# Eight conditioning jobs of layer 1 from VectorE to TensorE, TensorE held in program order through attention, and layer 0's scaled input kept in PSUM

## The chip, the cores and the metric

The kernel runs on one core of one Trainium2 chip. A time is the device time of one execution in microseconds; the kernel before took 926.71 us (median of 3 runs, 925.51 to 928.1). TensorE (PE), VectorE (DVE), ScalarE (ACT) and GpSimd (POOL) each run their own instructions strictly in the order in which they were laid down; SyncE (SP) issues the DMAs, also in order.

## The reference

One sample of 256 tokens of width 2048 goes through two layers. Every layer scales and shifts its normed input by vectors computed from a conditioning vector `c`, and gates its output by a third:

```python
mod = sc @ ada_w[layer] + ada_b[layer]            # sc = silu(c); 2048 x 6144
shift, scale, gate = jnp.split(mod[:, None, :], 3, axis=-1)
h = modulate(rmsnorm(x, norm_g[layer]), shift, scale)
...
k, v, q, za, glu, zb = jnp.split(h @ w_in, EV_SPLITS, axis=-1)      # layer 0
q = apply_rope(rmsnorm(q, ev_q_norm[e]), cos, sin)
k = apply_rope(rmsnorm(k, ev_k_norm[e]), cos, sin)
attn = latent_attention(q, k, v, kc, vc)          # kc, vc: the same weights on 256 context tokens
conv = conformer_conv(glu, ...)                   # 31 taps, LayerNorm, swish
mix = concatenate([attn * silu(za), conv * silu(zb)])
x = x + gate * (mix @ ev_w_out[e])
...
p = h @ od_w_in[o]                                # layer 1: spatial gating, SiLU gate
x = x + gate * ((spatial_gating(p[..., :2*SGU_W], ...) * silu(p[..., 2*SGU_W:])) @ od_w_out[o])
```

The output is the RMS-normed `x`.

## The kernel before, in words

All large products are done in two-part precision: weight and input are each split into a high part in a short format and the remainder, and three matmuls (high by high, high by low, low by high) stand for one. Weights stream from HBM in pieces of 512 KB. One piece is a **job** of kind W (`w_job`, line 347): a DMA into one of ten ring buffers `raw`; ACT makes the high part `whi` (line 361); POOL or DVE makes the remainder `wlo` (line 364; POOL for jobs 30 to 133, `P0` and `P1`); PE multiplies, 24 matmuls of 256 columns for a job of `w_rows` (lines 386 to 389), 12 of 512 columns for one of `w_cols` (409 to 411), 48 of 256 for keys and values (560 to 564). There are four `whi` and four `wlo` buffers, and a job is split up to four W jobs ahead. The sums stand in PSUM banks of tag `acc`, three of them, taken in turn; a helper, `part` (line 527), adds them into SBUF on DVE.

Jobs of kind A compute the conditioning vectors. Some run on PE (`adan_jobs`, line 289: matmuls against the 32-column `ccol`, ended by `ada_fin`, a copy on ACT, a transpose and an addition on DVE). The others run on DVE (`adat_jobs`, line 255): two SCALAR_TENSOR_TENSOR instructions on each 512 KB of transposed weights `traw`, against a copy of `c` in PSUM (line 274).

`make_h` (line 443) makes the layer's input for a group of rows: on DVE `ht` = x times scale times the norm's factor (line 453), on ACT the high part `h` = `ht` + shift (line 456), on DVE the remainder (line 460). `prep_x` does it for the tokens, `prep_c` for the context, in layer 0 in groups of 2 or 4 blocks of 128 rows; `prep1` does it for layer 1 once its norm is known.

Attention is a list of small **steps** (`side["attn"]`) put between the W jobs by `drain`. `rope_q` (line 753) takes the sum of squares of each query head (ACT, line 720), its reciprocal root (`rsqrt`, line 222), and rotates the unscaled queries on DVE (lines 709 to 714); the factor is applied later, in the soft-max. `attn_head` (line 773) is S = q k (line 776), the row maximum on DVE (779), its product with the factor (780), the exponential on ACT (782), a reciprocal (783) and a scaling on ACT (785). `attn_tr` (line 790) transposes that on PE (796) and copies it on ACT (797); `attn_pv` (line 801) multiplies with the values for two heads (807). S stands in the one bank of tag `S`, and once the flag `q` is set, every second one in an `acc` bank. The convolution's taps (line 626) are steps of a second list, all on DVE.

The order of each engine's instructions is not the program's: a scheduler lays them out from modelled times, and may move an instruction past others of its engine when the data allow it. `tc.high_priority()` and `tc.issue_after()` bend that; the DMAs alone are kept in the program's order.

Of the kernel before, what the change touches and what calls it, by code (L numbers as in the profile page):

```python
# [11 lines left out]
F32 = mybir.dt.float32  # L12
# [5 lines left out]
D = 2048  # L18
# [26 lines left out]
P2 = 4  # L45
# [32 lines left out]
NBLK = [(0, kind * D + k0 * 128, n * 128) for k0, n in GROUPS for kind in range(2)]  # L78
# [7 lines left out]
def backbone_kernel(  # L86
# [146 lines left out]


# [7 lines left out]
    def adat_pair(l, ca, cb_):  # L242

        ja, jb = adat_jobs(l, ca), adat_jobs(l, cb_)
        return [j for u in range(4) for js in (ja, jb) for j in js[4 * u : 4 * u + 4]]
# [9 lines left out]
    def adat_jobs(l, c0):  # L255

        js = []
# [3 lines left out]
        for u, q in enumerate(order):  # L261
            for t in range(4):
# [7 lines left out]
                def mm(jb=jb, t=t, q=q, u=u):  # L270
# [99 lines left out]
    def w_rows(jobs, src, kbs, h, post):  # L370
# [3 lines left out]
        for n, (kq, kts) in enumerate(parts):  # L374
            def mmf(jb, kq=kq, n=n, kts=kts):
# [3 lines left out]
                for kt in kts:  # L379
                    hh, hl = h(kq * 4 + kt)  # L380
                    k = kt - kts[0]
                    for b in range(2):
# [3 lines left out]
                        nc.tensor.matmul(o, wh, hh, start=(n == 0 and kt == kts[0] and b == 0), stop=False,  # L386
                                         skip_group_check=True)
                        nc.tensor.matmul(o, wh, hl, start=False, stop=False, skip_group_check=True)  # L388
                        nc.tensor.matmul(o, wl, hh, start=False, stop=end, skip_group_check=True)  # L389
# [4 lines left out]
    def w_cols(jobs, src_f, kbs, hs, post):  # L394
# [3 lines left out]
        for n, (kp, kts) in enumerate(parts):  # L398
            def mmf(jb, kp=kp, n=n, kts=kts):
# [3 lines left out]
                for i, (h, ch) in enumerate(hs):  # L403
                    for k, kt in enumerate(kts):
# [4 lines left out]
                        nc.tensor.matmul(accs[i], hh[:, sl], jb.hi[:, k, :], start=s0, stop=False)  # L409
                        nc.tensor.matmul(accs[i], hh[:, sl], jb.lo[:, k, :], start=False, stop=False)  # L410
                        nc.tensor.matmul(accs[i], hl[:, sl], jb.hi[:, k, :], start=False, stop=s1)  # L411
# [122 lines left out]
    turns = []  # L534

    def two_steps(first, second):

        side["attn"].append(first)
        if turns:
# [652 lines left out]
```

## Time and profile before

| | |
|---|---|
| median of 3 runs | 926.71 us |
| the profiled execution | 926.46 us, of which the profile's span is 924.7 us |
| PE busy | 872.9 us (94%) |
| DVE busy | 659.6 us (71%) |
| ACT busy | 457.9 us (50%) |
| POOL busy | 258.6 us (28%) |
| mean granted PE clock | 0.975 |

A busy time counts what an engine works, not what it waits. PE is near full in most of the span; it is not before 40 us, from 160 to 200, from 280 to 340, from 420 to 540 and behind 900 us. In a row of the windows view the numbers are busy microseconds and, in brackets, instructions of each engine in that stretch, then the granted PE clock as a share of full speed, the busy share of the DMA engines and GB/s. In the chain of waits each row is a piece of the path back from the last instruction: start, length, engine and what it wrote, with the line. In the view of groups, "busy, mean ns | idle before" stands behind each group of like instructions. "PEld" is PE's weight load.

### The profile page before, as it was taken

The numbers are of one execution on the slowest core, as the hardware profiler recorded it, in microseconds if no ns is written. First come the engines' busy times: TensorE is split into PE (matmuls) and PEld (weight loads), VectorE is DVE, ScalarE is ACT, GpSimd is POOL, SyncE is SP. The second block draws the span as 40 slices with busy tenths as digits, with TensorE's granted clock in tenths as the row PEclk, the third lists the DMA queues.
The fourth block names the chain that finished last, engine by engine and source line by source line (L and its number), as shares of the span: only waits on it lengthen the run. The fifth ranks groups of instructions, "written<-read, shape, count | busy, mean of one in ns | idle before, by whom it ended". The sixth has DMA issues, their size and how long they took to land.

```text
span 924.7 us, 17928 instructions
## 1 busy us (share of the span) xinstructions
PE 872.9 (94%) x7084; PEld 800.5 (87%) x7084; DVE 659.6 (71%) x1413; ACT 457.9 (50%) x648; POOL 258.6 (28%) x125
## 2 busy tenths in 40 slices
PE   5999999599998689999999899999999999999994
PEld 3798899599887578998999778998899999999994
DVE  2355684978887877895765299998988977554442
ACT  5643242347557668545544544455583544444441
POOL 0000023659875235686777520000000000000000
PEclk9999999799999899999999899999999999999998
DMA  9999999685776332678889579988887788755402
GB/s 355 406 389 352 363 338 365 252 286 173 233 247 217 121 114 91 205 249 298 312 311 342 175 277 410 409 312 304 311 281 225 250 282 281 218 185 174 137 1 91
DMA packets 66864, 239.06 MB, mean 259 GB/s; under 512 B 7502, under 2 KB 7768, under 8 KB 66268
## 3 DMA queue, kind: packets, MB, share of 16 engines
q1 hardware_dynamic: 66780, 237.92, 72.9%
q8 instruction: 55, 0.90, 0.4%
q14 instruction: 29, 0.24, 0.1%
HBM read 235.80 MB, written 2.10 MB: 257 GB/s over the span
## 4 chain that ended last, share of the span: by engine, by line
PE 76%; DVE 10%; DMA 10%; ACT 3%; issue 1%; POOL 0%; SPq 0%; DVEq 0%; POOLq 0%; ACTq 0%
PE acc L386 17%; PE acc L389 16%; PE acc L388 16%; DMA traw<-adat 7%; PE acc L409 4%; PE acc L410 4%; PE acc L411 4%; DVE traw L274 4%; PE ada L317 3%; PE acc L560 2%; PE acc L562 2%; PE acc L564 2%; DVE conv L626 1%; DMA braw<-ada 1%; PE rms L191 1%
## 5 line engine op out<-in xcount | busy, mean ns | idle before, releaser
L361 ACT ACTIVATE whi<-raw 128x1024 fp32r<-128x1024 f32 (+1 forms) x256 | 263.4, 1031 | 285.1 <-PE acc L388 140.4
L364 POOL TENSOR_TENSOR wlo<-raw,whi 128x1024 fp32r<-128x1024 f32 x104 | 250.9, 2425 | 283.3 <-ACT whi L361 145.4
L364 DVE TENSOR_TENSOR wlo<-raw,whi 128x1024 fp32r<-128x1024 f32 (+1 forms) x152 | 176.8, 1165 | 83.3 <-ACT whi L361 81.7
L274 DVE SCALAR_TENSOR_TENSOR traw<-traw,cbp 128x512 f32<-128x512 f32 x256 | 165.3, 682 | 56.0 <-DMA traw<-adat 52.7
L386 PE MATMUL acc<-h,whi 128*128 128x256 f32 x512 | 152.4, 299 | 8.0 <-DVE gaT L532 6.7
L388 PE MATMUL acc<-h,whi 128*128 128x256 f32 x512 | 149.3, 293 | 0.4 <-DVE h L460 0.4
L389 PE MATMUL acc<-h,wlo 128*128 128x256 f32 x512 | 148.0, 290 | 1.6 <-POOL wlo L364 1.6
L388 PE MATMUL acc<-h1l,whi 128*128 128x256 f32 x512 | 145.2, 284 | 0.0
L389 PE MATMUL acc<-h1h,wlo 128*128 128x256 f32 x512 | 145.0, 283 | 0.0
L386 PE MATMUL acc<-h1h,whi 128*128 128x256 f32 x512 | 145.0, 283 | 0.0
L626 DVE SCALAR_TENSOR_TENSOR conv<-gaT,small,conv 128x241 f32<-128x241 f32 (+14 forms) x240 | 114.6, 478 | 5.2
L386 PEld LDWEIGHTS acc<-h,whi 128*128 128x128 f32 x512 | 100.6, 197 | 14.1 <-issue 10.3
L389 PEld LDWEIGHTS acc<-h,wlo 128*128 128x128 f32 x512 | 100.5, 197 | 4.1 <-issue 2.0
L388 PEld LDWEIGHTS acc<-h,whi 128*128 128x128 f32 x512 | 100.7, 197 | 3.5 <-issue 2.6
L388 PEld LDWEIGHTS acc<-h1l,whi 128*128 128x128 f32 x512 | 98.2, 192 | 0.1
L386 PEld LDWEIGHTS acc<-h1h,whi 128*128 128x128 f32 x512 | 98.2, 192 | 0.1
L389 PEld LDWEIGHTS acc<-h1h,wlo 128*128 128x128 f32 x512 | 98.2, 192 | 0.0
L389 PE MATMUL acc<-m1h,wlo 128*128 128x256 f32 x256 | 73.1, 286 | 0.0
L386 PE MATMUL acc<-m1h,whi 128*128 128x256 f32 x256 | 72.4, 283 | 0.0
L388 PE MATMUL acc<-m1l,whi 128*128 128x256 f32 x256 | 72.4, 283 | 0.0
L389 PEld LDWEIGHTS acc<-m1h,wlo 128*128 128x128 f32 x256 | 49.1, 192 | 2.9 <-issue 2.9
L411 PE MATMUL acc<-whi,h1l 128*128 128x512 f32 x128 | 51.1, 400 | 0.0
(235 smaller groups left out, 1649.1 us busy)
## 6 DMA issues: line engine op xcount, KB each, us to landing
traw<-adat SPq DMA_DIRECT2D x128, 512.0 KB, 5.0
raw<-w_out SPq DMA_DIRECT2D x64, 512.0 KB, 4.0
raw<-w_uz SPq DMA_DIRECT2D x64, 512.0 KB, 4.9
araw<-ada SPq DMA_DIRECT2D x56, 512.0 KB, 6.9
raw<-w_gate SPq DMA_DIRECT2D x56, 512.0 KB, 5.1
raw<-w_v SPq DMA_DIRECT2D x32, 512.0 KB, 5.1
raw<-w_q SPq DMA_DIRECT2D x16, 512.0 KB, 4.1
raw<-w_gate SPq DMA_DIRECT2D x16, 256.0 KB, 11.0
```

The costliest lines, as they stand in the source:

```text
L274: nc.vector.scalar_tensor_tensor(out=jb.raw[:, k, :], in0=jb.raw[:, k, :], scalar=1.0, in1=cbq["t"], op0=ALU.mult, op1=ALU.mult, accum_out ...
L317: nc.tensor.matmul(st8["p"][32 * g : 32 * g + 32, :w], ccol[:, kb, :], jb.raw[:, a, q * w : (q + 1) * w], start=kb < 4 // nq, stop=kb >= N ...
L361: nc.scalar.activation(hv, jb.raw, AF.Copy)
L364: eng.tensor_tensor(out=jb.lo.rearrange("p a b -> p (a b)"), in0=jb.raw, in1=hv.bitcast(F32), op=ALU.subtract)
L386: nc.tensor.matmul(o, wh, hh, start=(n == 0 and kt == kts[0] and b == 0), stop=False, skip_group_check=True)
L388: nc.tensor.matmul(o, wh, hl, start=False, stop=False, skip_group_check=True)
L389: nc.tensor.matmul(o, wl, hh, start=False, stop=end, skip_group_check=True)
L409: nc.tensor.matmul(accs[i], hh[:, sl], jb.hi[:, k, :], start=s0, stop=False)
L410: nc.tensor.matmul(accs[i], hh[:, sl], jb.lo[:, k, :], start=False, stop=False)
L411: nc.tensor.matmul(accs[i], hl[:, sl], jb.hi[:, k, :], start=False, stop=s1)
L560: nc.tensor.matmul(o, hh[:, sl], jb.hi[:, k, :], start=kq == kqs[0] and k == 0 and c == 0, stop=False, skip_group_check=True)
L626: nc.vector.scalar_tensor_tensor(out=o, in0=y, scalar=w, in1=o, op0=ALU.mult, op1=ALU.add)
```

## The change

Four things are changed together.

1. **Conditioning.** The shift vector's blocks 8 to 11 of layer 1 (columns 1024 to 1535) are no longer computed on DVE. They were 8 of the 32 DVE jobs of `ada1b` (`ts=range(2, 4)` leaves t = 2 and 3) and are now 8 jobs of `adan_jobs` on PE, behind the hook of `prep1(0)`, the norm of layer 1.
2. **PE's order.** Matmuls and transposes of W jobs and of attention go through `inorder`, which ties each to the one before it, from the first query job up to layer 1's norm. Attention's list is rewritten for that: one `unit` between two W jobs holds S of head n, the value product of two earlier heads and the transpose of head n - 3, all with high priority, and the two transposes of queries are steps of their own. The first two W jobs behind the queries take no step (`rest`).
3. **Scaled queries.** `rope_q` scales the queries in PSUM on ACT (four instructions for 4 heads), as the keys already were; the rotation works in place with one SBUF temporary at a time. The soft-max loses the factor: the maximum is negated in the reduction, and line 780 goes.
4. **Scaled input.** In layer 0 `make_h` puts `ht` in a PSUM bank (tag `m`, two banks) in place of SBUF.

```diff
-NBLK = [(0, kind * D + k0 * 128, n * 128) for k0, n in GROUPS for kind in range(2)]
+NBLK = [(0, kind * D + k0 * 128, n * 128) for k0, n in GROUPS for kind in range(2)] + [(1, 1024, 512)]
...
+    def inorder(op, *args, **kw):
+
+        with tc.issue_after(pe["last"]) if pe["on"] and "last" in pe else nullcontext():
+            i = op(*args, **kw)
+        pe["last"] = i.ins
...
-            t = tmp.tile([128, 2, T], F32, tag="t2", name="ht", bufs=TB)
+            if m == 4:
+                t = bank("ht").rearrange("p (a b) -> p a b", a=2)
+            else:
+                t = tmp.tile([128, 2, T], F32, tag="t2", name="ht", bufs=TB)
...
-        at["rq"][i, cg] = head_rstd(src, 4, "qss", HD ** -0.5)
+        r = head_rstd(src, 4, "qss", HD ** -0.5)
+        for h in range(4):
+            nc.scalar.activation(src[:, h * 128 : (h + 1) * 128], src[:, h * 128 : (h + 1) * 128], AF.Copy, scale=r[:, h : h + 1])
...
-        nc.vector.tensor_reduce(out=mx[:, 0:1], in_=S, axis=AX.X, op=ALU.max)
-        nc.vector.tensor_scalar(out=mx[:, 1:2], in0=mx[:, 0:1], scalar1=rq, scalar2=-1.0, op0=ALU.mult, op1=ALU.mult)
+        nc.vector.tensor_reduce(out=mx[:, 1:2], in_=S, axis=AX.X, op=ALU.max, negate=True)
...
+        def unit(n):
+
+            if n < len(todo):
+                attn_head(*todo[n])
+            if n > AD and (n - AD) % 2 == 0:
+                attn_pv(*todo[n - AD - 1])
+            if AD <= n < len(todo) + AD:
+                attn_tr(*todo[n - AD])
+        for n in range(len(todo) + AD + 1):
             if n == len(todo) // 2:
-                half = len(out)
...
+                out.append(("q", both(turn_q, 1)))
+            out.append(lambda n=n: unit(n))
+        return out + [("za", attn_gate), lambda: attn_fin(0), lambda: attn_fin(1)]
...
-    segs = [body, qa + kv[0] + za[:4] + qb, kv[1] + za[4:] + [za_ready], z_part(1) + [conv_tail], [need("attn")] + o0a, [need("conv")] + o0b]
+    segs = [body, [hook(lambda: pe.__setitem__("on", True))] + qa + za[:2] + kv[0] + za[2:4] + qb + [hook(lambda: st.__setitem__("rest", 2))], za[4:8] + kv[1] + za[8:] + [za_ready], z_part(1) + [conv_tail], [need("attn")] + o0a, [need("conv")] + o0b]
...
-    ada1b = adat_pair(1, 1024, D + 1024)
-    plan += [hook(lambda: prep1(0)), hook(sgu_const)]
+    ada1b = adat_pair(1, 1024, D + 1024, range(2, 4))
+    plan += [hook(lambda: pe.__setitem__("on", False)), hook(lambda: prep1(0))] + adan_jobs(1, 1024, 512) + [hook(sgu_const)]
```

Three places in the built order show where instructions went. The first is DVE at the last `prep_x` and `prep_c` of layer 0 (blocks 12 to 15; line 453 or 470 is `ht`, 460 or 477 the remainder of tokens (`h_2267`) and context (`hc`), 274 or 287 conditioning, 532 or 549 the emptying of an `acc` bank). Before:

```order
L453 SCALAR_TENSOR_TENSOR ht<-xT_71,modv_133,rB_223 128x256 x4
L453 SCALAR_TENSOR_TENSOR ht<-cT_325,modc,rBc 128x256 x4
L274 SCALAR_TENSOR_TENSOR traw,adat<-traw,cbp 128x512 x2
L532 TENSOR_TENSOR kv_sb<-acc,kv_sb 128x2x256
L460 SCALAR_TENSOR_TENSOR h_2267<-ht,modv_133,h_2267 128x256
L274 SCALAR_TENSOR_TENSOR traw,adat<-traw,cbp 128x512 x2
L460 SCALAR_TENSOR_TENSOR h_2267<-ht,modv_133,h_2267 128x256 x3
L460 SCALAR_TENSOR_TENSOR hc<-ht,modc,hc 128x256
L532 TENSOR_TENSOR gaT<-acc,gaT 128x512
```

And in the changed kernel, from the second pair of token blocks on:

```order
L470 SCALAR_TENSOR_TENSOR ht<-xT_71,modv_133,rB_223 128x256 x2
L287 SCALAR_TENSOR_TENSOR traw,adat<-traw,cbp 128x512 x3
L549 TENSOR_TENSOR gaT<-acc,gaT 128x512
L287 SCALAR_TENSOR_TENSOR traw,adat<-traw,cbp 128x512
L477 SCALAR_TENSOR_TENSOR h_2267<-ht,modv_133,h_2267 128x256 x4
L287 SCALAR_TENSOR_TENSOR traw,adat<-traw,cbp 128x512 x4
L470 SCALAR_TENSOR_TENSOR ht<-cT_325,modc,rBc 128x256
L549 TENSOR_TENSOR gbT<-acc,gbT 128x512
L470 SCALAR_TENSOR_TENSOR ht<-cT_325,modc,rBc 128x256 x3
L477 SCALAR_TENSOR_TENSOR hc<-ht,modc,hc 128x256 x4
L287 SCALAR_TENSOR_TENSOR traw,adat<-traw,cbp 128x512 x2
L549 TENSOR_TENSOR gaT<-acc,gaT 128x512
```

The first emptying of `gaT` now stands ahead of the remainders, the second (the last row) behind those of the context, and the context's `ht` behind the tokens' remainders.

The second is ACT around the second group of queries (`sqj` are the squares, line 767 the new scaling, 222 or 223 the root, 782 or 787 the exponential, 785 or 790 the scaling behind it, 797 or 802 and 815 or 820 copies of transposes and values). Before, the exponentials of S stand between the parts of the query norm, each with a load of its function table:

```order
L720 ACTIVATE sqj,qss<-acc 128x128
L782 ACT_TABLE_LOAD
L782 ACTIVATE P,mx<-S,mx,qss 128x512
L223 ACT_TABLE_LOAD
L223 ACTIVATE qss<-qss,epsc 128x4
L361 ACTIVATE whi<-raw 128x1024
L785 ACTIVATE P<-P,mx 128x512
L815 COPY mixA<-O 128x2x128
L361 ACTIVATE whi<-raw 128x1024
L782 ACT_TABLE_LOAD
L782 ACTIVATE P,mx<-S,mx,qss 128x512
```

In the changed kernel the rows from the fourth square of the second half on; ahead of them stand, behind the last query matmul, the squares x4, a table load, the root, a square, `whi`, a square, a copy of a transpose, a square, a scaling:

```order
L730 ACTIVATE sqj,qss<-acc 128x128
L767 ACTIVATE acc<-acc,qss 128x128
L222 ACTIVATE qss<-qss,epsc 128x4
L767 ACTIVATE acc<-acc,qss 128x128 x2
L375 ACTIVATE whi<-raw 128x1024
L767 ACTIVATE acc<-acc,qss 128x128 x4
L375 ACTIVATE whi<-raw 128x1024 x2
L787 ACT_TABLE_LOAD
L787 ACTIVATE P,mx<-S,mx 128x512
L790 ACTIVATE P<-P,mx 128x512
L787 ACTIVATE P,mx<-S,mx 128x512
```

The exponential of head 6 now stands behind the whole query norm; on PE, S of head 6 comes right behind the last query job, then three W jobs (72 matmuls), then S of head 7, in the same bank.

The third is PE at layer 1's norm (`rms` the sums of squares, `csum_p` and `csum_b` the steps to its factor, `bs_p` constants of the gating unit, `ada` the moved conditioning matmuls). Before:

```order
L191 MATMUL rms_5553<-sq_6086,onesD 32x256 x2
L207 MATMUL csum_p<-q_126,csum 128x1 x2
L212 MATMUL csum_b<-ident,rs 128x128 x2
L170 MATMUL bs_p<-rowh,sel 128x128
L171 MATMUL bs_p<-rowl,sel 128x128
```

Changed:

```order
L331 MATMUL ada_6150<-araw,ccol 32x128 x39
L190 MATMUL rms_5553<-sq_6078,onesD 32x256 x2
L331 MATMUL ada_6150<-araw,ccol 32x128 x22
L206 MATMUL csum_p<-q_126,csum 128x1 x2
L331 MATMUL ada_6150<-araw,ccol 32x128 x3
L211 MATMUL csum_b<-ident,rs 128x128 x2
L347 MATMUL adat<-ident,adar 128x128
L238 MATMUL acc<-whi,h1h 128x512
```

All 64 conditioning matmuls stand in the gaps between the steps of the norm, and the eight `bs_p` moved behind the first four matmuls of the next job.

More of the change, by code (lines that the diff above doesn't have):

```diff
@@ L44 @@
 L1 = 2
-P2 = 4
 NF = 3
@@ L240, in backbone_kernel, with adat_pair @@
         pool = False
-    def adat_pair(l, ca, cb_):
-        ja, jb = adat_jobs(l, ca), adat_jobs(l, cb_)
-        return [j for u in range(4) for js in (ja, jb) for j in js[4 * u : 4 * u + 4]]
+    def adat_pair(l, ca, cb_, ts=range(4)):
+        ja, jb = adat_jobs(l, ca, ts), adat_jobs(l, cb_)
+        return [j for u in range(4) for js in (ja[u], jb[u]) for j in js]
     cbq = {"q": None}
@@ L253, in cb_part, with adat_jobs @@
             nc.vector.tensor_copy(cbq["t"], cb[:, q * 512 : (q + 1) * 512])
-    def adat_jobs(l, c0):
-        js = []
+    def adat_jobs(l, c0, ts=range(4)):
+        js = [[] for _ in range(4)]
         n = TSET.index((l, c0))
@@ L261, in adat_jobs @@
         for u, q in enumerate(order):
-            for t in range(4):
+            for t in ts:
                 jb = Job()
@@ L385, in mmf @@
                         end = n == len(parts) - 1 and kt == kts[-1]
-                        nc.tensor.matmul(o, wh, hh, start=(n == 0 and kt == kts[0] and b == 0), stop=False,
+                        matmul(o, wh, hh, start=(n == 0 and kt == kts[0] and b == 0), stop=False,
                                          skip_group_check=True)
-                        nc.tensor.matmul(o, wh, hl, start=False, stop=False, skip_group_check=True)
-                        nc.tensor.matmul(o, wl, hh, start=False, stop=end, skip_group_check=True)
+                        matmul(o, wh, hl, start=False, stop=False, skip_group_check=True)
+                        matmul(o, wl, hh, start=False, stop=end, skip_group_check=True)
                 if n == len(parts) - 1:
@@ L532, in part @@
             nc.vector.tensor_tensor(out=dst, in0=a, in1=dst if prev is None else prev, op=ALU.add)
[L534 to L539, printed above, removed]
-            side["attn"].append(turns.pop(0))
-        turns.append(second)
     def kv_part(kqs):
@@ L828, in attn_steps, with both @@
     def attn_steps():
-        out, half = [], 0
+        def both(f, *args):
+            return lambda: [f(i, *args) for i in range(2)]
+        out = [both(turn_k), lambda: [turn_k(i) for i in (2, 3)], both(turn_q, 0)]
         todo = [(kvh, c, hq) for kvh in range(NKV) for c in range(2) for hq in range(4)]
-        for n in range(len(todo) + AD):
-            if n == len(todo) // 2:
-                half = len(out)
-            if n < len(todo):
-                out.append(lambda n=n: attn_head(*todo[n]))
-            if n >= AD:
-                out.append(lambda n=n: attn_tr(*todo[n - AD]))
-                if (n - AD) % 2 == 1:
-                    out.append(lambda n=n: attn_pv(*todo[n - AD]))
-        out.append(("za", attn_gate))
-        out += [lambda: attn_fin(0), lambda: attn_fin(1)]
-        return out[:half], out[half:]
+        def unit(n):
[6 more added lines that the diff above has]
+        for n in range(len(todo) + AD + 1):
+            if n == len(todo) // 2:
+                out.append(("q", both(turn_q, 1)))
+            out.append(lambda n=n: unit(n))
+        return out + [("za", attn_gate), lambda: attn_fin(0), lambda: attn_fin(1)]
     def hm(kb):
@@ L1024, in drain @@
             s = side[key].pop(0)
-            (s[1] if isinstance(s, tuple) else s)()
+            with tc.high_priority() if key == "attn" else nullcontext():
+                (s[1] if isinstance(s, tuple) else s)()
             k += 1
@@ L1074, in backbone_kernel @@
         if j.kind == "W":
-            j.pool = P0 <= nw < P1 and nw % 4 < P2
+            j.pool = P0 <= nw < P1
             nw += 1
@@ L1107, in backbone_kernel @@
             for key in ("attn", "conv"):
+                if key == "attn" and st.get("rest"):
+                    st["rest"] -= 1
+                    continue
                 ahead = [n for k, n in deadline.items() if k == key and n > p]
@@ L1110, in backbone_kernel @@
                 for _ in range(math.ceil((PACEA if key == "attn" else PACE) * len(side[key]) / max(1, left))):
-                    if side[key] and isinstance(side[key][0], tuple) and side[key][0][0] == "za" and "za" not in st:
+                    if side[key] and isinstance(side[key][0], tuple) and side[key][0][0] not in st:
                         break
```

78 lines of the change are left out of this document (39 added, 39 removed).

## The prediction

> **What bounds the kernel now.** I read the page's slices first, then the windows around each stretch where PE is not full, then the chain of waits in the two worst, then the groups for durations. In the windows the first pair of numbers is PE's busy time and its matmuls; PEclk and the DMA share stand at the end.
>
> ```profile
> 160.00:200.00 40.00, 30.45 (x218) 29.90 (x216) 33.52 (x60) 15.25 (x20) 23.36 (x10) 0.83 0.73 269
> 200.00:220.00 20.00, 20.00 (x169) 20.00 (x168) 18.10 (x44) 14.24 (x37) 14.29 (x15) 1.00 0.61 195
> 200.00:420.00 220.00, 207.78 (x1372) 185.13 (x1374) 186.19 (x461) 136.67 (x230) 138.80 (x70) 0.97 0.58 191
> 280.00:340.00 60.00, 47.78 (x267) 37.75 (x266) 48.06 (x126) 40.91 (x71) 24.89 (x11) 0.89 0.46 150
> 540.00:900.00 360.00, 360.00 (x2671) 342.48 (x2670) 277.11 (x494) 180.64 (x209) 2.40 (x1) 1.00 0.74 256
> ```
>
> PE is the bound: from 540 to 900 us it has no idle time at all, so nothing that is taken from DVE there can show. The losses lie earlier. At 200 to 220 us PE does 169 matmuls of 256 columns in 20 us, 0.118 us each. From 160 to 200 us it does 218, worth 25.8 us: **14.2 us are lost**, of which 9.55 are idle and the rest is slow clock (0.83). So each idle microsecond cost 1.49. From 280 to 340 us shapes mix and no such count can be made: 12.2 us are idle, the clock (0.89) is worth up to 6.6 more; scaled like the first stretch (14.2 of 9.55 + 6.8) I take **16.5 lost**, bounds 12.2 and 18.8.
>
> The chain of waits in the first stretch, start and length:
>
> ```profile
> 161.54 2.29 DVE modc L344
> ...
> 165.04 3.17 DVE ht L453 x8
> ...
> 169.95 2.50 DVE h L460
> 172.45 1.21 DVE traw L274 x4
> 173.66 6.30 DVE h L460 x3
> 179.97 2.48 DVE hc L460
> 182.45 0.61 DVE gaT L532
> ```
>
> PE waits for none of the remainders here, but for an `acc` bank that `gaT` empties, and `gaT` stands behind five remainders on DVE. Those take 2.1 to 2.5 us each; the same instruction takes a fifth elsewhere. What differs is POOL, which runs five `wlo` at that time:
>
> ```profile
> 169.81 12.35 POOL L364 TENSOR_TENSOR wlo<-raw,whi 128x1024 fp32r<-128x1024 f32 x5 [6.00 <-ACT whi L361]
> ...
> L460 DVE SCALAR_TENSOR_TENSOR h<-ht,modv,h 128x256 fp32r<-128x256 f32 x16 | 16.3, 1056 | 0.1
> L274 DVE SCALAR_TENSOR_TENSOR traw<-traw,cbp 128x512 f32<-128x512 f32 x256 | 165.3, 682 | 56.0 <-DMA traw<-adat 52.7 <-issue 1.4 <-POOL kr L714 0.7
> L453 DVE SCALAR_TENSOR_TENSOR ht<-cT,modc,rBc 128x256 f32<-128x256 f32 x16 | 6.7, 477 | 0.0
> L453 DVE SCALAR_TENSOR_TENSOR ht<-xT,modv,csum_b 128x256 f32<-128x256 f32 x8 | 3.2, 475 | 1.1 <-PE csum_b L212 1.1
> ```
>
> `traw` at 172.45, with one input in SBUF and one in PSUM (`cbp`), keeps its pace while POOL works; the remainder, with both in SBUF, doesn't. One operand in PSUM costs DVE nothing by itself: 475 ns with `csum_b` (PSUM), 477 with `rBc` (SBUF). The Trainium skill (SBUF — State Buffer, "Who interferes with whom") says so as a rule: a VectorE instruction with two SBUF inputs waits for a GpSimd instruction that reads SBUF, one with a single SBUF input does not. By that rule, the trace agrees, 2.50 us for the first remainder and 1.21 for the `traw` pieces behind it, the new remainder is free; `ht`, with two inputs in SBUF, is not (a rival below).
>
> In the second stretch, who PE waited for (us in total, times, longest), and the pieces that PE and ACT work there:
>
> ```profile
> PE S L776 <- ACT P L782: 3.9, 2, 2.3
> PE acc L776 <- ACT z0T L601: 3.0, 1, 3.0
> PE S L776 <- ACT qT L770: 2.6, 1, 2.6
> PE O L807 <- ACT PT L797: 2.6, 1, 2.6
> ...
> 347.23 0.44 PE ptp L796 x4
> 350.78 0.86 PE S L776 x2
> 352.83 1.73 PE O L807 x8
> ...
> L361 ACT ACTIVATE whi<-raw 128x1024 fp32r<-128x1024 f32 x53 | 56.0, 1057 | 49.0 <-PE acc L388 24.4 <-issue 9.7 <-POOL wlo L364 6.5
> L785 ACT ACTIVATE P<-P,mx 128x512 f32<-128x512 f32 x16 | 11.6, 723 | 4.5 <-DVE mx L783 4.5
> L797 ACT COPY PT<-ptp 128x512 f32<-128x512 f32 x16 | 9.3, 582 | 3.2 <-PE ptp L796 3.1
> L782 ACT ACTIVATE P<-S,mx,qss 128x512 f32<-128x512 f32 x11 | 8.5, 776 | 14.2 <-DVE mx L780 14.2
> L782 ACT ACT_TABLE_LOAD x6 | 7.7, 1283 | 0.1
> L720 ACT ACTIVATE sqj<-acc 128x128 f32<-128x128 f32 x16 | 4.4, 274 | 0.9 <-PE acc L411 0.6
> L720 ACT ACTIVATION_READ_ACCUMULATOR sqj<-acc 128x1 f32 x16 | 3.2, 197 | 0.0
> ...
> 244.98 0.28 ACT L720 ACTIVATE sqj<-acc 128x128 f32<-128x128 f32 x1 [0.62 <-PE acc L411]
> 257.89 0.41 DVE L714 TENSOR_TENSOR qr<-rp,rp 128x256 f32<-128x256 f32 x1
> ```
>
> Every wait is for ACT, whose queue alternates between exponential, root and SiLU with 1.28 us of table load at each turn.
>
> **The change part by part.** *Scaled input in PSUM.* The remainder then reads one input from SBUF. The five on the chain (2.50 + 6.30 + 2.48 = 11.3 us) would take some 0.4 us each, 2 us: the 0.48 of `ht` less overlap (3.17 for eight). What is late next? By the new order, with the trace's durations from the transposes at 160 us: `ht` at 164.4 to 167, `gaT` 169.5, the tokens' remainders until 171.8. PE's third job waits about 1.2 us for its `wlo`, and the sixth for the `acc` bank that the second `gaT` empties behind the context's remainders: near 180, 1.4 us of wait, if the context's `ht` (both inputs still in SBUF) is not held up by POOL; near 184, 5.8 us, if POOL's `wlo` hold two of them for 2 us each. Left over: 1.2 + 1.4 = 2.6 us, or (1.2 + 5.8) with clock, some 9. The gain is 11.5 or 5; I take **8**, between them, since POOL worked in most, not all, of that time (23.36 of 40 us).
>
> *PE in order, units, scaled queries.* A unit with its W job fills PE for 24 x 0.118 + 0.86 + 0.44 + 1.73/2 = 5.0 us. ACT needs for the same 1.06 + 0.78 + 0.72 + 0.58, with an accumulator's reading (0.2) and half of a value copy about 3.5 us, and for every fourth job two table loads more, 4.2 us. So PE need not wait in the plain run of units, and the seven units of the first key head have one table load in all. Four places remain. (a) The first queries: from the first square to the last rotation it took 13.3 us (244.98 to 258.3); eight scalings of about 0.28 (by the square's 274) add 2; PE has 15 us of other work ahead of the transposes: 0.5 us. (b) S of head 7 needs the bank of head 6, whose exponential stands behind the second query norm: 8 squares of 0.4 us (274 and 197 ns, overlapping), 4 `whi`, 8 scalings, two roots and a copy of a transpose some 1.2 (0.58 for the copy, the roots an estimate as for a square), two table loads 2.6, the exponential 0.8: 3.2 + 4.2 + 2.2 + 1.2 + 2.6 + 0.8 = 14.2 us from the last query matmul. PE has S, a transpose and 72 matmuls until then: 1.3 + 8.5 = 9.8. It waits 4.4 us, 6.5 with its clock (x 1.49). (c) A new `z` sum wants the `acc` bank which the SiLU empties: a table load 1.3, the SiLU about as long as the copy of 582 ns, a `whi` ahead of it 1.06, less the 1.3 of S and transpose that PE has: 1.5. (d) Others, chosen: 1. Together **9.5 against 16.5: gain 7**. Bounds: nothing waits but (b), gain 12; every unit waits as before, gain 0. The skill's rule on the clock (TensorE: Matmul & The Clock Gate, "What's actually happening") speaks against this part: the array falls to half speed after an idle window of about 3.4 us. By that rule, (b) would cost at most 1.7 us beyond its idle time, an estimate, and the sum be 0.4 us lower than with my 2.1; the clock of 0.83 where 9.55 of 40 us were idle agrees.
>
> ```profile
> L780 DVE TENSOR_SCALAR mx<-mx,qss 128x1 f32<-128x1 f32 x16 | 3.1, 204 | 0.0
> DVE traw L274 <- DMA traw<-adat: 8.0, 9, 1.3
> ...
> 32.68 0.79 PE ada L317 x22
> 38.71 1.01 PE ada L317 x32
> PE rms L191 <- ACT sq L877: 1.6, 1, 1.6
> PE csum_b L212 <- DVE rs L224: 0.6, 1, 0.6
> PE csum_p L207 <- ACT csum L204: 0.5, 1, 0.5
> ```
>
> *Convolution.* DVE loses 16 x 0.204 = 3.3 us with line 780 and must finish its taps on time, as PE sums them right behind attention. From 200 to 420 us DVE is busy for 186 of 220; if PE is 15 us sooner, it has 205 for 183, 89%, with 8.0 us of waiting for the data of nine `traw` on top. The last tap may come late: 0 to 5 us, I take **1.5 of loss**.
>
> *Eight jobs on PE.* 64 matmuls at 1.01 us for 32 are 2.0 us. They stand in waits for the norm of 1.6, 0.5 and 0.6 us, 2.7 together. **Nothing**, while their data is there: without that cover 2 us, and if the eight ring buffers that they hold until then delay the next weights, 2 more. DVE's 16 instructions less (16 x 0.68 = 10.9 us) lie in the stretch without a PE wait and give nothing. The `bs_p` that leave the gap fill the wait for the remainder behind four matmuls: 0, bounds -1 and +1.5.
>
> Sum: 926.5 (profiled execution; span 924.7 and 1.8 around it; median 926.7) - 8 - 7 + 1.5 = **913 us**.
>
> **The rivals.** *The lock moves on.* The context's `ht`, and the next group's, still have two SBUF inputs; each start behind a `wlo` costs up to 2 us, as line 460 now. For it: POOL will have `wlo` queued when they start; against: `ht` ran at 0.47 in every row, because its ACT successors held the `whi` back. First gain 5 in place of 8: 926.5 - 5 - 7 + 1.5 = 916 us. The Trainium skill's rule on two SBUF inputs (SBUF — State Buffer, the section named above) would have it so.
>
> *DVE becomes the bound.* Its taps are laid down with waits for S and DMA among them; if none of its 34 idle us go, PE waits at the sums of the convolution for what it won in attention: 926.5 - 8 = 918.5.
>
> *Slower.* In program order PE cannot step over an S whose bank is taken. If maximum (0.69), `whi` (1.06), scaling (0.72), exponential (0.78) and on DVE a `traw` pair (1.5) with its DMA wait (1.1) stand in a row, the bank is free after 5.85 us; PE's cover from S to S is 5.0 - 0.86 = 4.1. 16 units wait 1.75 each, 28 us, with (b) 34.4 against 16.5: 926.5 + 17.9 - 8 + 1.5 = 938 us. It decides from 1 us per unit on. Against it: DVE has idle time there, and units have high priority.
>
> *No effect.* The waits return elsewhere, for weights: 926. Against it: a DMA share of 0.61 behind the first stretch.
>
> **How the numbers follow.** Forecast 48%, lock 20%, DVE 17%, no effect 8%, slower 7%. A measurement can tell 0.3% (2.8 us) from no change. Forecast, lock and DVE are faster: 0.85; same 0.08; slower 0.07. The range: 901 (the larger ends, 11.5 + 12, with some loss) to 923 leaves out no effect, slower, and a few per cent below.
>
> **What would show it.** Remainders of layer 0 near 0.48 us in the groups; 160 to 200 us with PE above 35 us busy; one wait of S for the exponential of 4 to 5 us behind the second queries; no table load between exponentials before that; the sums of the convolution with PE waiting 1 to 2 us; PE full behind the norm. Wrong, if remainders stay long, if many S wait, or if PE waits for DMA at the norm.

## The result, and the profile after

The changed kernel takes 919.75 us (median of 20 runs, 915.92 to 928.9), the kernel before beside it 927.5 us (20 runs, 924.71 to 933.34). The ratio is 0.9923, with a 95% interval of 0.9903 to 0.9942: some 7 us faster, where 13.5 were predicted. The profiled execution of after took 921.4 us (span 919.5), 1.65 above its median; that of before, 1.04 below its own. So the two traces lie 5.1 us apart and the medians 7.75. Single executions scatter by 3 us and more, and small effects are better read stage by stage than from the totals.

The two traces cut at the same TensorE work, in us between the first starts of the matmuls named (PE's rows in order of time); "hidden products" are the first matmuls behind layer 1's norm:

| stage | before | after | difference | predicted |
|---|---|---|---|---|
| start to the first output matmul of layer 0 | 416.6 | 401.7 | -14.9 | -8 - 7 |
| output matmuls of layer 0 (convolution beside them) | 105.7 | 109.3 | +3.6 | +1.5 |
| norm of layer 1, to the first hidden product | 7.0 | 7.1 | +0.1 | 0 |
| first 32 high-by-high hidden products | 27.1 | 30.6 | +3.5 | 0 |
| the next 111 us of them | 111.4 | 111.4 | 0 | 0 |
| the stretch with the gating matmuls | 145.6 | 148.3 | +2.7 | 0 |
| the rest, to the last matmul | 101.8 | 102.2 | +0.4 | 0 |

The 15 us that were to be won up to the end of attention were won. Ten were lost again behind it, where 1.5 had been allowed for.

The windows of after, PE's busy time and matmuls first, PEclk and the DMA share at the end:

```profile
160.00:200.00 40.00, 35.31 (x278) 34.56 (x277) 35.27 (x80) 18.70 (x29) 27.62 (x12) 0.96 0.90 336
280.00:340.00 60.00, 56.09 (x366) 49.01 (x365) 54.01 (x129) 43.94 (x85) 28.65 (x12) 0.94 0.47 150
298.60:305.30 6.70, 5.87 (x13) 4.02 (x14) 6.70 (x15) 1.50 (x3) 2.47 (x2) 0.50 0.81 290
520.40:527.20 6.80, 6.80 (x20) 5.62 (x21) 6.80 (x15) 3.02 (x7) 2.51 (x1) 0.50 1.03 413
527.20:534.00 6.80, 6.80 (x31) 5.52 (x30) 6.80 (x7) 2.38 (x3) 5.07 (x2) 1.00 0.97 383
660.00:700.00 40.00, 37.80 (x313) 37.23 (x312) 33.07 (x67) 22.88 (x24) 0.00 (x0) 1.00 0.78 250
```

From 160 to 200 us PE does 278 matmuls where it did 218, and from 280 to 340 us it idles 3.9 us where it idled 12.2. But from 660 to 700 us, inside the stretch that had no idle time, it now idles 2.2. Of the signs that the prediction named, one is plainly missing: PE is not full behind the norm.

The groups on DVE that the first term of the sum rests on (a line's mean in ns stands behind its busy time):

```profile
L477 DVE SCALAR_TENSOR_TENSOR h<-ht,modv,h 128x256 fp32r<-128x256 f32 x16 | 6.8, 475 | 1.1 <-ACT h L473 1.1
L470 DVE SCALAR_TENSOR_TENSOR ht<-cT,modc,rBc 128x256 f32<-128x256 f32 x16 | 13.5, 883 | 0.1
L477 DVE SCALAR_TENSOR_TENSOR h1l<-ht,modv,h1h 128x256 fp32r<-128x256 f32 x16 | 13.2, 878 | 0.0
```

The tokens' remainder went from 1056 to 475 ns, and the context's `ht` from 477 to 883: the hold-up has moved one instruction on.

Who PE waited for, from 240 us to the end of attention (402), then from 400 to 530, then from 640 to 720 us (total, times, longest):

```profile
PE S L238 <- ACT P L787: 4.6, 2, 3.9
PE acc L238 <- ACT z0T L609: 1.3, 1, 1.3
PE O L238 <- ACT PT L802: 1.1, 1, 1.1
PE ktp L238 <- ACT kT L759: 1.0, 1, 1.0
...
PE cmean L190 <- ACT gaT L637: 2.3, 1, 2.3
PE acc L238 <- DVE mBl L455: 1.6, 1, 1.6
PE bs_p L169 <- DVE modv L354: 1.1, 1, 1.1
PE acc L238 <- ACT h1h L473: 1.0, 1, 1.0
PE acc L238 <- ACT mBh L454: 0.7, 1, 0.7
...
PE sgu L963 <- DVE mixed L971: 1.4, 1, 1.4
PE sgu L963 <- ACT v L936: 0.7, 1, 0.7
```

In attention stand the waits that were foretold, S of head 7 with 3.9 us first. Behind it are three places that were not there before: the convolution's sums and last parts (2.3, 1.6 and 0.7; before, one wait of 1.0 for `cvar`), the broadcasts `bs_p` behind the norm, and the gating matmuls `sgu`, where PE had waited for nothing.

The output matmuls in two windows, first before, then after:

```profile
416.60:522.40 105.80, 103.09 (x840) 96.02 (x838) 59.21 (x156) 51.83 (x66) 77.06 (x33) 1.00 0.84 296
401.70:511.00 109.30, 104.75 (x840) 97.09 (x838) 62.78 (x164) 51.95 (x66) 75.97 (x33) 0.98 0.84 287
```

For the same 840 rows PE idles 4.6 us in place of 2.7 and works 1.7 us longer, as its clock stands at half for 3.4 us there (411.1 to 414.6) and never did before. Together these are the 3.6 us.

### The profile page after: what moved, and what is told of

It is laid out like the page before. It is cut to its first block, busy times and chain, and to the rows that moved or that the text cites. A ratio compares the mean times of both kernels' runs of the same rounds, so it can differ in the third digit from the quotient of the medians.

```text
span 919.5 us, 18133 instructions
## 1 busy us (share of the span) xinstructions
PE 871.7 (95%) x7213; PEld 802.5 (87%) x7213; DVE 646.9 (70%) x1366; ACT 455.5 (50%) x661; POOL 257.9 (28%) x125
## 4 chain that ended last, share of the span: by engine, by line
PE 79%; DMA 9%; DVE 8%; ACT 2%; issue 1%; POOL 0%; SPq 0%; DVEq 0%; POOLq 0%; ACTq 0%
PE acc L238 70%; DMA traw<-adat 7%; DVE traw L287 3%; PE ada L331 3%; PE O L238 2%; PE rms L190 1%; DVE ht L470 1%; DMA araw<-ada 1%; PE S L238 1%; PE ptp L238 1%; DVE wlo L378 1%; PE sgu L963 1%; DMA cin<-ccol 1%; ACT whi L375 0%; DVE xT L1017 0%
## 5 line engine op out<-in xcount | busy, mean ns | idle before, releaser
L287 DVE SCALAR_TENSOR_TENSOR traw<-traw,cbp 128x512 f32<-128x512 f32 x240 | 154.9, 682 | 64.5 <-DMA traw<-adat 63.1
L238 PE MATMUL acc<-h,whi 128*128 128x256 f32 x1024 | 193.7, 290 | 5.0 <-DVE gaT L549 2.8
L238 PEld LDWEIGHTS acc<-h,whi 128*128 128x128 f32 x1024 | 162.1, 195 | 10.0 <-ACT whi L375 4.1
L238 PE MATMUL acc<-h,wlo 128*128 128x256 f32 x512 | 145.5, 285 | 1.5 <-POOL wlo L378 1.5
L238 PE MATMUL acc<-whi,h 128*128 128x256 f32 (+1 forms) x256 | 68.1, 346 | 1.3 <-ACT z0T L609 1.3
L238 PEld LDWEIGHTS acc<-whi,h 128*128 128x128 f32 x256 | 44.6, 190 | 8.3 <-ACT z0T L609 1.7
L238 PE MATMUL acc<-whi,h1h 128*128 128x512 f32 x128 | 50.7, 401 | 1.0 <-ACT h1h L473 1.0
```

The costliest lines, as they stand in the source:

```text
L238: i = op(*args, **kw)
L287: nc.vector.scalar_tensor_tensor(out=jb.raw[:, k, :], in0=jb.raw[:, k, :], scalar=1.0, in1=cbq["t"], op0=ALU.mult, op1=ALU.mult, accum_out ...
```

## The experiments

The first theory, A, was that each part keeps what it wins and the eight blocks on TensorE make the loss; the rival, B, that VectorE is the second bound, so that time won earlier is taken back behind attention. The medians have 6 to 12 runs each; ratios are to the kernel before. The variant without the blocks on TensorE is called *no_jobs*, as its run.

**The parts one by one.** *ht_only* is the kernel before with one edit, *jobs_only* with the other; *no_jobs* and *order_only* take the same out of the changed kernel. Program order, units and scaled queries (2 and 3 of the change) stay together in all runs.

```diff
 # ht_only: before, and (order_only: the reverse, and jobs taken out)
+            if m == 4:
+                t = bank("ht").rearrange("p (a b) -> p a b", a=2)
 # no_jobs: after, and (jobs_only: the reverse, on before); the blocks' entry in NBLK goes too
-    ada1b = adat_pair(1, 1024, D + 1024, range(2, 4))
-    plan += [..., hook(lambda: prep1(0))] + adan_jobs(1, 1024, 512) + [hook(sgu_const)]
+    ada1b = adat_pair(1, 1024, D + 1024)
+    plan += [..., hook(lambda: prep1(0)), hook(sgu_const)]
```

> The kernel before with the scaled input of layer 0 in PSUM and nothing else. Theory A (each part keeps what it wins; the loss is made by the eight blocks on TensorE): the stretch from 160 to 200 us loses 7 us in place of 14.2, and the time falls by the same 7.3 us, to 920. Theory B (VectorE's convolution and the conditioning data are the second bound, so time won earlier is taken back at the convolution's sums, in the second half of the output matmuls and at the gating matmuls): the stretch wins the 7.3 us, but 3 to 6 of them are gone at the end, 923 to 926.

> The kernel before with TensorE in program order through attention (and the new units and rotation), without the scaled input in PSUM and without the eight blocks on TensorE. Theory A: the 7 us of attention less 3.5 at the convolution and the output matmuls: 924. Theory B: the same won, but as the first stretch has given nothing, VectorE is not yet late, and less is taken back: 921 to 922.

> The changed kernel with the eight conditioning blocks back on VectorE. Theory A: the broadcasts behind the norm no longer stand behind the result of the eight blocks, the 3.4 us lost in the first 20 us behind the norm and the 2.7 us at the gating matmuls go: 914 to 916. Theory B: VectorE has 10.9 us more to do, the waits at the gating matmuls grow and eat what the norm wins: 919 to 923.

> The kernel before with the eight conditioning blocks on TensorE and nothing else. Theory A: the blocks' 128 passes (4.1 us) fill the 2.7 us of waits at the norm, and the broadcasts behind them wait for their result, 3 us or more lost: 930 to 932. Theory B: the blocks are free at the norm, and VectorE has 10.9 us less to do in a stretch where TensorE does not wait for it: 927.

Measured: *ht_only* 919.48 us, ratio 0.9917 (0.9889 to 0.9946); *order_only* 921.88, 0.9937 (0.9915 to 0.9959); *no_jobs* 914.86, 0.9873 (0.984 to 0.9906); *jobs_only* 936.54, 1.0094 (1.0079 to 1.011). The two earlier parts together bring 12.9 us; the blocks cost 4.9 on top of them and 8.8 alone. The 4.9 are the less certain figure: the intervals of after (0.9903 to 0.9942) and *no_jobs* (0.984 to 0.9906) still touch. *ht_only* and *no_jobs* came out as theory A has it, *order_only* as B; *jobs_only* cost more than either had allowed (930 to 932 and 927). The changed kernel is faster in spite of the eight blocks, and *no_jobs* is the change without them.

The stages of all runs, cut as in the table above (one execution each; the plain 111 us and the rest are left out, they stay within 1.3 us):

| run | to output | output | norm | first 32 | gating |
|---|---|---|---|---|---|
| before | 416.6 | 105.7 | 7.0 | 27.1 | 145.6 |
| ht_only | 409.1 | 109.1 | 7.5 | 27.7 | 147.9 |
| order_only | 406.3 | 108.4 | 6.1 | 29.0 | 147.7 |
| no_jobs | 402.8 | 109.1 | 7.7 | 27.4 | 146.4 |
| after | 401.7 | 109.3 | 7.1 | 30.6 | 148.3 |
| jobs_only | 416.4 | 107.4 | 7.1 | 30.5 | 150.9 |
| bs_first | 402.1 | 111.4 | 7.1 | 29.2 | 150.1 |
| gate_early | 404.6 | 111.4 | 7.1 | 31.0 | 145.5 |
| dve_relief | 401.9 | 107.8 | 7.3 | 26.8 | 145.3 |
| fewer_taps | 403.4 | 103.2 | 6.3 | 28.0 | 146.1 |
| held | 403.8 | 109.5 | 7.1 | 31.5 | 145.7 |
| held_bs | 399.9 | 108.0 | 7.1 | 29.0 | 145.7 |
| rest4 | 399.3 | 110.2 | 7.3 | 28.4 | 145.3 |
| rest4_pace | 399.8 | 114.9 | 7.7 | 27.4 | 145.3 |
| pool_less | 403.3 | 108.9 | 7.1 | 30.6 | 150.2 |
| held_bs_pool | 402.5 | 105.7 | 7.1 | 33.9 | 145.7 |

Kernels that are alike up to the first output matmul differ there by 399.9 to 404.6: that is the scatter. Both theories hold a part. The output matmuls take 2 to 6 us longer in nearly all kernels that come to them early, with or without the blocks (B). *rest4_pace* loses 9; *held_bs_pool* loses nothing, as PE idles 2.5 us there and its clock stays full. The blocks add some 3 us to the first 32 products, and 2 to 5 to the gating against before and *no_jobs* (A); but *ht_only* and *order_only* lose 2 at the gating without them.

**Where the blocks cost.** PE's rows in after around the norm, in order of time:

```profile
511.17 2.27 PE L331 MATMUL ada<-araw,ccol 128*32 128x128 f32 x75
513.18 0.40 PE L190 MATMUL rms<-sq,onesD 128*32 128x256 f32 x1
513.27 0.39 PE L331 MATMUL ada<-araw,ccol 128*32 128x128 f32 x5
...
513.49 0.28 PE L331 MATMUL ada<-araw,ccol 128*32 128x128 f32 x2
...
513.64 1.47 PE L331 MATMUL ada<-araw,ccol 128*32 128x128 f32 x40
...
515.58 0.42 PE L331 MATMUL ada<-araw,ccol 128*32 128x128 f32 x6
516.29 0.68 PE L211 MATMUL csum_b<-ident,rs 128*128 128x128 f32 x4 [0.29 <-DVE rs L223]
516.81 0.27 PE L347 MATMUL adat<-ident,adar 128*128 128x128 f32 x1
518.09 0.50 PE L238 MATMUL acc<-whi,h1h 128*128 128x512 f32 x1 [1.00 <-ACT h1h L473]
...
518.89 0.40 PE L238 MATMUL acc<-wlo,h1h 128*128 128x512 f32 x1
520.36 0.47 PE L169 MATMUL bs_p<-rowh,sel 10*128 10x128 f32 x1 [1.07 <-DVE modv L354]
...
522.25 0.80 PE L238 MATMUL acc<-whi,h1l 128*128 128x512 f32 x1
```

The same in *no_jobs*:

```profile
513.74 0.63 PE L190 MATMUL rms<-sq,onesD 128*32 128x256 f32 x4 [1.63 <-ACT sq L886]
...
516.49 1.19 PE L211 MATMUL csum_b<-ident,rs 128*128 128x128 f32 x4 [0.64 <-DVE rs L223]
517.61 0.47 PE L169 MATMUL bs_p<-rowh,sel 10*128 10x128 f32 x1
...
519.51 0.80 PE L238 MATMUL acc<-whi,h1h 128*128 128x512 f32 x1
...
520.95 0.63 PE L238 MATMUL acc<-wlo,h1h 128*128 128x512 f32 x1
521.38 1.91 PE L952 MATMUL rsum<-wsT,ones 128*128 128x512 f32 x2
522.30 1.42 PE L238 MATMUL acc<-whi,h1l 128*128 128x512 f32 x1
```

There are 75 + 5 + 2 + 40 + 6 = 128 rows of `ada` for 64 matmuls: a float32 matmul stands as two rows, and PE is busy with them for 4.4 us. The gap hides them all the same (7.1 us against 7.7). What they push out is the eight `bs_p`, which in *no_jobs* lie in the gap. Now these wait for the bank that the blocks' result is read from (line 354), so that 3.4 us (518.89 to 522.25) pass between the fourth product and the fifth, 1.35 in *no_jobs* (520.95 to 522.30), where `rsum` fills part of it.

At the gating, who DVE waited for most from 640 to 720 us, in before, after and *no_jobs*:

```profile
DVE traw L274 <- DMA traw<-adat: 2.8, 4, 0.9
```

```profile
DVE traw L287 <- DMA traw<-adat: 11.1, 8, 2.2
```

```profile
DVE traw L287 <- DMA traw<-adat: 3.9, 4, 1.4
```

In DVE's row the gate's first eight conditioning jobs stand behind 54, 56, 58, 59, 61, 63, 64 and 65 weight remainders in after, behind 56, 58, 60, 62, 63, 64, 67 and 68 in *no_jobs*. The scheduler, with 16 instructions fewer on DVE, laid them down one to three jobs earlier, while their transfers follow the ring of buffers. Four kernels try this:

```diff
 # bs_first: after, and
-    ... adan_jobs(1, 1024, 512) + [hook(sgu_const)]
+    ... [hook(sgu_const)] + adan_jobs(1, 1024, 512)
 # gate_early: after, and
-G1 = 0
+G1 = 8
 # dve_relief: no_jobs, and for these eight blocks
+    w = 16 if (l, c0) == (1, 1024) and t < 2 else 512
...
-    out=jb.raw[:, k, :], in0=jb.raw[:, k, :], scalar=1.0, in1=cbq["t"], ...
+    out=jb.raw[:, k, :w], in0=jb.raw[:, k, :w], scalar=1.0, in1=cbq["t"][:, :w], ...
 # held: after, and for the first 16 jobs of the gate, behind the seventh-last weight remainder
-    with after("crit"):
+    late = l == 1 and c0 >= 2 * D and u < 2
+    with tc.issue_after(wlos[-7]) if late else after("crit"):
```

> The changed kernel with the broadcasts for the gating (bs_p) put ahead of the eight blocks in the program, so that on TensorE they stand in the norm's gap again, not behind the blocks' result and the first four matmuls. If the 3.2 us lost in the first 20 us behind the norm come from that wait (2.6 us between the first four matmuls and the broadcasts, and the broadcasts themselves), they go: about 916.5. Rival: what is lost there is the 128 passes (4.1 us) of the blocks themselves, which fill a gap of 2.7 us only, and the order behind them does not matter: 919.5, as the changed kernel.

> The changed kernel with eight of the gate's conditioning jobs moved from the second half of layer 1's first matmuls to the first half, where the eight blocks have left VectorE free. If the gating matmuls wait because VectorE has been put ahead of the data there (10.1 us of waits for conditioning data between 640 and 700 us against 2.3 without the blocks on TensorE), these waits shrink below 4 us and the time falls by 1.8 to 2.7 us: 917 to 918. Rival: the data are late since the transfers of the eight blocks sit in the ring of buffers ahead of the norm; then nothing changes: 919.5 to 920.

> The variant with the eight blocks on VectorE (914.9 us), but each of their 16 instructions works on 16 of its 512 columns; the rest of that product is left out. TensorE, the transfers and the ring of buffers stay as they were. If VectorE's work there is hidden and less of it gives nothing: 914.9. If less work on VectorE is itself what puts it ahead of its data and makes the gating matmuls wait: 917 to 918, slower with less work. If VectorE's time was on the path after all: below 913.

> The changed kernel with the first sixteen conditioning jobs of the gate kept behind the same number of weight remainders in VectorE's row as in the variant with the eight blocks on VectorE (56, 58, 60 ... in place of 54, 56, 58, 59 ...). If their earlier place is what makes VectorE wait for their data between 640 and 720 us (11.1 us, against 3.9 in that variant) and the gating matmuls behind it wait, the waits shrink below 5 us, the stretch of the gating matmuls takes 48 us in place of 50.4, and the time is 917 to 918. Rival: the data themselves come later since the blocks' transfers were moved ahead; then VectorE waits as long, and the time stays at 919.5 to 920.5.

Measured: *bs_first* 920.63 us, ratio 0.9916 (0.9885 to 0.9948); *gate_early* 920.71, 0.9932 (0.9908 to 0.9956); *dve_relief* 913.46, 0.9862 (0.9831 to 0.9893); *held* 918.57, 0.9882 (0.9852 to 0.9913). In total *bs_first* and *gate_early* can't be told from after, so the 916.5 and 917 to 918 that were expected did not come, and the interval of *held* still touches that of after. By the stages (one execution each) each does its own: with *bs_first* the first 32 products take 29.2 in place of 30.6, with *gate_early* the gating stretch 145.5 in place of 148.3. *dve_relief*, which leaves out most of those products, refutes the simple form of my theory: less work on VectorE alone makes no wait (145.3). *held* ties nothing but those jobs on DVE, and DVE's waits for the data are gone, with PE's at `sgu`. But the scheduler lays the other rows anew as well: from 658 to 737 us PE and ACT have another order too, and the first `sgu` starts 17.1 us into the gating stretch in place of 15.8. This is what DVE waited for most from 640 to 720 us:

```profile
DVE wlo L381 <- ACT whi L378: 5.1, 3, 2.9
...
```

The four kernels with the blocks on TensorE and the gate's jobs left where the scheduler put them take 148.3 to 150.9 us there; the repaired ones 145.5 and 145.7, those without the blocks 145.3 to 147.9. DVE's waits for the data are 11.1 to 13.3 us in the first group, none in *held*. So the place of the jobs in VectorE's row makes these waits, and moving the jobs back takes them away. That PE loses its time through them is likely, but not shown apart from the new place of the `sgu`. It is not the only way to lose time there either: *ht_only* and *order_only* have nearly the order of *no_jobs*, wait 4.8 and 4.4 us for the data, and take 147.9 and 147.7. How much of the 2 to 5 us is the blocks' alone is open.

**The convolution.** *fewer_taps* leaves out ten of the 31 taps, and with them a part of the result; *rest4* gives PE more work ahead of S of head 7; *rest4_pace* also lays the taps down faster. All stand on *no_jobs*.

```diff
-        for n in range(t0, t1):
+        for n in range(t0, min(t1, 21)):          # fewer_taps
-    hook(lambda: st.__setitem__("rest", 2))
+    hook(lambda: st.__setitem__("rest", 4))       # rest4, rest4_pace
-PACE = 1.4
+PACE = 2.0                                        # rest4_pace
```

> The variant with the eight blocks on VectorE (914.9 us), with 21 of the convolution's 31 taps; the other ten are left out, 80 instructions of 0.48 us, 38 us of VectorE. If VectorE bounds the convolution and the output matmuls behind attention, the two halves of those matmuls take again the 105.7 us that they took before (109.1 now), and attention may gain too: 911 or less. If the 3.4 us are lost for ScalarE, the transfers or the order alone: 914 to 915.

> The variant with the eight blocks on VectorE (914.9 us), with four weight jobs in place of two between the second query products and the next head's S. The wait of S for the exponential behind the second query norm (4.1 us, and 6.8 us of half clock behind it) should shrink to 0 to 1 us, and attention by 4 to 6 us. If it comes through to the end: 909 to 911. If VectorE bounds the convolution behind it, as the run with fewer taps has it, what attention wins is lost there: 913 to 915.

> The same with the convolution's taps laid down faster beside attention (pace 2.0 in place of 1.4). If VectorE's time bounds the stretch, nothing is won by another order: as the run without it, within 1.5 us. If the taps only stand too late in VectorE's row: 3 us less than that run, 907 to 910.

Measured: *fewer_taps* 910.54 us, ratio 0.9812 (0.9783 to 0.9841); *rest4* 915.22, 0.9846 (0.9813 to 0.9879); *rest4_pace* 916.96, 0.987 (0.984 to 0.99). PE's waits from 400 to 515 us in *no_jobs*, and the same in *fewer_taps*:

```profile
PE acc L238 <- DVE mBl L455: 2.3, 1, 2.3
PE rms L190 <- ACT sq L886: 1.6, 1, 1.6
PE acc L238 <- ACT mBh L454: 1.1, 1, 1.1
PE cmean L190 <- ACT gaT L637: 1.1, 1, 1.1
```

```profile
PE rms L190 <- ACT sq L886: 2.1, 2, 1.6
PE csum_b L211 <- DVE rs L223: 0.6, 1, 0.6
...
```

With less DVE work the three waits of the convolution go, and the output matmuls fall from 109.1 to 103.2 us. *rest4* is the counterpart: the long wait of S goes, attention ends 3.5 us earlier than in *no_jobs* (399.3, at the low end of the scatter), a wait of `acc` for `qr` on DVE (2.3) appears, and the total is that of *no_jobs*. Another pace wins nothing. The taps themselves show why. In before the last of them ends at 416.9 us, 0.3 behind the first output matmul. In *ht_only* PE comes to these matmuls 7.5 us sooner, and the last tap ends at 417.1. In after it ends at 410.5, 8.8 behind the first output matmul; in *fewer_taps* at 342.0. So VectorE's taps bound what comes behind attention.

**What is left at the norm.** Of the 3.2 us between after and *no_jobs* in the first 32 products, *bs_first* explains 1.4. In what is left, 1.8, PE idles 0.7 us (*no_jobs*: none), and its clock stands at half for 6.8 us of these products in place of 5.3: *no_jobs* has the other 5 us at half clock in the norm's gap, where PE has little to do. The eight blocks' data also hold eight of the ten ring buffers, so the hidden products' weights come later (the first is issued at 498.1 us, in *no_jobs* at 483.1), and one of GpSimd's weight remainders slips behind the norm, onto the first remainders of the scaled input. After, and then *no_jobs*, in order of time:

```profile
520.22 3.76 DVE L477 SCALAR_TENSOR_TENSOR h1l<-ht,modv,h1h 128x256 fp32r<-128x256 f32 x4
520.26 2.65 POOL L378 TENSOR_TENSOR wlo<-raw,whi 128x1024 fp32r<-128x1024 f32 x1 [7.90 <-ACT whi L375]
```

```profile
520.86 1.67 DVE L477 SCALAR_TENSOR_TENSOR h1l<-ht,modv,h1h 128x256 fp32r<-128x256 f32 x4
```

Four remainders take 3.76 us in place of 1.67.

```diff
 # held_bs: held and bs_first; pool_less: after, and; held_bs_pool: held_bs, and
-P1 = 134
+P1 = 131
```

> The same, and the broadcasts for the gating ahead of the eight blocks. If the two costs of the eight blocks on TensorE are the broadcasts that they push out of the norm's gap (29.2 against 30.6 us for the first 32 of the hidden products with that alone) and VectorE's waits: 915.5 to 916.5, near the variant without the blocks (914.9). If TensorE's slow clock, which the blocks move from the gap onto the work behind it, is a part of its own: 917.

> The changed kernel with the last three weight remainders of GpSimd on VectorE, so that GpSimd is idle while the first remainders of layer 1's scaled input run. If GpSimd's remainder holds them up (four took 3.76 us, 1.67 in the variant without the blocks on TensorE), they take 0.48 us each again and the first 32 hidden products start 1.5 to 2 us sooner (28.5 to 29 in place of 30.6 us): about 918. If TensorE's slow clock makes the loss: 30.6 us and 919.5 as before.

> The changed kernel with all three repairs: broadcasts ahead of the blocks, the gate's first sixteen jobs kept back on VectorE, and GpSimd out of the way behind the norm. If these are all that the eight blocks cost: 27.5 us for the first 32 hidden products (29.0 with two repairs) and 914.5 to 915, as without the blocks on TensorE. If the slow clock is a part of its own: 29 us and 916.4.

Measured: *held_bs* 916.36 us, ratio 0.9857 (0.9816 to 0.9899); *pool_less* 922.44, 0.9941 (0.9922 to 0.996); *held_bs_pool* 921.83, 0.9923 (0.9885 to 0.9961), from seven runs, with an eighth at 926.53 left out. Two repairs bring the change with the blocks close to the one without them (0.9873), and clear of after. The third repair failed in both runs: 918 and 914.5 to 915 had been expected. Without GpSimd in the way the remainders are fast again, in *pool_less*

```profile
L477 DVE SCALAR_TENSOR_TENSOR h1l<-ht,modv,h1h 128x256 fp32r<-128x256 f32 x16 | 6.8, 480 | 0.0
```

but the first 32 products still take 30.6 us, as the `bs_p` wait covers it. In *held_bs_pool* other waits took its place:

```profile
PE rsum L956 <- DMA wsT<-wsT: 2.1, 1, 2.1
PE acc L238 <- DVE h1l L481: 1.4, 1, 1.4
```

Its first 32 products take 33.9 us: PE idles 3.5 us, and its clock stands at half for 10.2 us (in *held_bs* 1.8 and 3.4). Whether that long a block of slow clock comes from the edit or from the execution, no run tells.

The last 1.6 us between *held_bs* (29.0) and *no_jobs* (27.4) are idle time. PE is busy for 27.2 and 27.4 us of these products, at a mean clock of 0.94 and 0.90, so the slow clock is not the cause. PE waits 1.8 us for remainders of the scaled input (`h1l`) in *held_bs* and for nothing in *no_jobs*, where `rsum` stands in front of the first product that needs one. No run moves `rsum` alone.

## Why the prediction was half right

- **Scaled input in PSUM, 8 predicted: right.** *ht_only* reaches the output matmuls 7.5 us sooner and its median is 8.2 lower. The two fit less well than they look: its profiled execution (926.2 us) is the slowest of its six, and its trace, 924.4 us, loses nearly all of the 7.5 again behind attention. The rival that the lock moves on came true in part: the context's `ht` took up to 2.6 us (its line's durations, min, median and max in ns),

```profile
L470 DVE SCALAR_TENSOR_TENSOR ht<-cT,modc,rBc x16: 480/484/2625, 55.0 to 178.6; 128x256 f32<-128x256 f32 x16
```

  and PE waited for the sum behind it, as the row of the start in PE's order shows:

```profile
182.85 0.77 PE L238 MATMUL acc<-h,whi 128*128 128x256 f32 x2 [2.75 <-DVE gaT L549]
```

  So the gain lies between the bounds of 5 and 11.5. The Trainium skill (SBUF — State Buffer, "Who interferes with whom") has a VectorE instruction with two SBUF inputs contend with a GpSimd instruction that reads SBUF; the trace agrees, with 2.6 us against 0.48, while GpSimd's `wlo` ran from 168.6 to 178.4.
- **Attention, 7 predicted: right.** The first stage is 14.9 us shorter, 15 predicted with the term above. That the two meet to a tenth is luck, as kernels alike up to there differ by 4.7. The program order with the scaled queries won 10.3 us up to the output matmuls in *order_only*, and 6.3 on top of *ht_only* (in *no_jobs*). The wait of S was 3.9 (4.4 predicted), the `z` sum's 1.3 (1.5). In the 6.7 us at half clock around the start of S (PEclk 0.50 in the window above) PE worked 5.9, so the wait costs some 2.9 us more, where I had 2.1. The Trainium skill (TensorE: Matmul & The Clock Gate, "What's actually happening") has the clock halved from an idle window of about 3.4 us on; the trace agrees, with 3.9 us of idle ahead of S. The "at most 1.7 us" that I had worked out from that rule was too low.
- **Convolution, 1.5 predicted: mis-sized.** It lost 3.4 to 3.6 us, inside the bounds of 0 to 5: 1.9 us more idle time, as foretold, and 1.7 for the half clock, which the term left out. Busy shares hid it: VectorE is 64 us busy of 110 there, but the taps end late.
- **"Eight jobs on PE ... Nothing": the step that failed.** Measured 4.9 us, 8.8 alone. The matmuls themselves lie in the gap, as said, though PE is busy with them for 4.4 us and not 2.0: the 32 rows of 1.01 us that I took for 32 matmuls were 16. Two costs were put at nothing. The `bs_p` that leave the gap do not just "fill the wait for the remainder behind four matmuls": they wait for the blocks' own result, 1.4 us by *bs_first*, the upper end of the bounds (-1 and +1.5) where 0 had been taken. And "DVE's 16 instructions less ... give nothing" was true of time and wrong of order: the scheduler moved later jobs forward into waits for their data (11.1 us in place of 3.9), and the gating took 1.9 us more in after than in *no_jobs*. A third, the ring buffers that delay the next weights, was named and not counted; the weights came 15 us later, and what is left at the norm lies there in part.
- **"From 540 to 900 us it has no idle time at all, so nothing that is taken from DVE there can show."** It could not show as a gain; it showed as a loss. A stage without waits can get some.

Without the blocks the forecast, 913, lies 1.9 us from what *no_jobs* did (914.86), which is what the convolution was mis-sized by. The lower end of the range was added wrongly: 926.5 - 11.5 - 12 is 903, and some loss makes it higher, not 901.

## What to carry to other kernels

Where a scheduler lays down the rows, an instruction taken away moves its successors too: compare each engine's order far behind the edit, above all the instructions that wait for transfers. Work that is put into a gap pushes out the work that lay there, and what came behind the gap may now wait for the newcomer's buffer or bank. When several edits go together, run each alone: here one of three cost over a third of what the two others won (4.9 of 12.9 us; 8.8 when run alone).

## What the runs showed of the hardware

- Float32 matmuls stand as two rows each in the trace (128 rows for 64 `ada`, and `rms` x4 for two); their transposes (`adat`) and the matmuls of the split formats stand as one. Counts of rows are no counts of instructions.
- The slow clock comes as a block, not as a rate over the idle time: 520.4 to 527.2 us at 0.50 in after, full right behind. A product of 512 columns starts every 0.43 us in it (523.27, 523.70, 524.13) and every 0.23 behind it (527.62, 527.85, 528.08).
- Small matmuls in the gap did not keep that block away: PE idles 1.3 of the norm's 7.1 us in after, and the block starts 2.3 us behind the first product all the same. In *no_jobs*, which idles 2.7 of 7.7, it starts 5.0 us ahead of the first product.
